# Inversion regions side by side, attention keys evacuated plainly, products spread anew, and decays in two matmuls, in a one-core hybrid encoder kernel

## The chip, the cores and the metric

The kernel runs on one core of a Trainium2 chip. The engines that matter are TensorE (PE, with its weight loads shown as PEld), VectorE (DVE), ScalarE (ACT), GpSimd (POOL) and SyncE (SP), whose queue issues nearly all DMAs. Each engine takes its instructions in order. The metric is the device time in microseconds, the median over runs.

## The reference

One encoder layer on a prompt of 1024 tokens and a sample of 256 (1280 tokens, NB = 10 blocks of 128, or 20 chunks of 64), model width 1024, float32. The normed input goes through one projection, whose columns feed three groups of heads; their gated outputs are concatenated and projected back:

```python
xn = rms_norm(h, norm_g)
proj = xn @ w_in          # a_qkv, gates, beta, alpha | b_q, b_k, b_v | c_q, c_k, c_v
qkv = silu(centred_dwconv(a_qkv, conv_w))                 # 5 taps
o_a = gated_delta_rule(...) + flip_t(gated_delta_rule(flipped ...))   # 6 heads, both directions
o_b = retention(...) + flip_t(retention(flipped ...))     # 6 heads, both directions
o_c = window_attention(q, k, v, sink)                     # 4 heads, 2 KV heads, window 128, ALiBi, sink
mix = concat([norm(o_a) * silu(gate_a), norm(o_b) * silu(gate_b), o_c * silu(gate_c)])
h = h + mix @ w_out
h = h + (p @ w_ple) * sigmoid(h @ w_pg);  y = rms_norm(h, final_g)

def gated_delta_rule(q, k, v, beta, g):                   # chunks of 64
    decay = cumsum(g)
    gamma = exp(where(incl, decay_i - decay_j, -inf))
    t_mat = where(strict, (k*beta) @ k.T * gamma, 0) + eye(64)
    u, w = triangular_solve(t_mat, [v*beta, k*beta*exp(decay)])
    # scan over chunks: state, o = step(state, u, w, q @ k.T * gamma, ...)
```

## The kernel before, in words

**Dense products.** A product takes 128 columns of `w_in` against all 1280 tokens. Activations and weights are split in a high and a low part (`xh`, `xl`, `whi`, `wlo`), and each of the 5 groups of 256 tokens takes 8 × 3 matmuls, 120 in all. There are nine for the convolution and 21 others, named in lists: `cq0 cq1 ck cv` for attention, `q k v` 0 to 2 for retention, and the numbers 0 to 7 for gate columns (`GCOL`). Each is evacuated in blocks of 512, 512 and 256 tokens. `plain` copies a block to a slot of `ot`, a tile of eight slots [128, tokens] used again and again. `evg` makes a gate: ACT copies the block to `sz` (L477), makes its sigmoid in three activations into `sg` (L99–L101), DVE multiplies them, and for gates 0 to 5 a DMA on SP stores `sg` in DRAM (`gd`). `evk` splits the keys `ck` out of PSUM into `kst`, two tiles with high and low part, six ACT copies and six DVE subtractions.

**Preparation.** `prep_stream` runs over the token blocks 9 to 0. For each it makes a Gram matrix, transposes the keys and, for each direction d, the decays: `SD[i]`, four rows of selectors, spreads the decay values in `dj` over 128 rows, and for i = 0 a further matmul with an identity (`identR`) adds the mask `MB[d]` of −1e30. Six exponentials on ACT follow (`ge`), then products on DVE and stores to DRAM (`agd`, `ad`, `l2d`).

**Inversion.** After five blocks (group g = 1, then g = 0) `invert(g)` inverts the triangles of 32 × 32 of both directions at once: it loads them from `agd` into two slots of `ot`, `IREG[d]`, runs 31 steps of DVE operations (L88, `ot<-ot` on 120 rows), ends with a memset (L426), and stores the inverses (`yd`). The access pattern of each operation spans both regions, with the stride between them.

**Joins and scan.** A join reads five chunks' inverses back (`yn`, `an`), transposes them (`xn`, L671), and completes the 64 × 64 inverses with two rounds of small matmuls (`sb<-xn,an`, then `p1s`, then `sb<-yn,p1s`). There are four for each group; its tiles have one buffer. Joins 0 to 3 belong to g = 1, joins 4 to 7 to g = 0. Then 20 scan steps for both directions (`step`, ending in `os`, L752), and norms of finished blocks.

**What sets the order.** The streams yield estimated times, and `spread` and `weave` interleave their emission: preparation and both inversions with the products in `PP`; then `PA`; then joins and scan, woven with `fill`: ten blocks of attention with `PB`, then retention (`kv(p)`, `av(p)`) with the products in `RS`. A list scheduler with a simulated timeline (`TCARGS`) makes each engine's final queue from that emission order, the dependences and the buffers. When everything is emitted up to the last scan step, the final products with `w_out`, `w_pg` and `w_ple` follow.

```python
PP = ["cq0", "cq1", 6, 7, 3, 4, 0, 5, "cv", 1, 2]
PA, PB = ["ck"], ["q0", "k0"]
RS = [["v0"], ["q1"], ["k1", "v1"], ["q2"], ["k2", "v2"], [], []]
...
for _ in spread((10 * T_PREP + 2 * 32.2, prep_stream()), length(PP)):
...
yield from spread((10 * T_AT, attn_stream()), length(PB))
```

Of the kernel before, what the change touches and what calls it, by code (L numbers as in the profile page):

```python
# [33 lines left out]
KG, MG = (), ()  # L34
AO = tuple(range(NB))
X2, SPN = 4, 0
PP = ["cq0", "cq1", 6, 7, 3, 4, 0, 5, "cv", 1, 2]
PA, PB = ["ck"], ["q0", "k0"]
RS = [["v0"], ["q1"], ["k1", "v1"], ["q2"], ["k2", "v2"], [], []]
T_PREP = 10.0  # L40
YB, VB, KB, QB = 1, 2, 1, 1
QLB = 1
SLOPE = [2.0 ** (-2 * (h + 1)) for h in range(4)]
NEG = -30000.0
XB = 6
# [7 lines left out]
def encoder_kernel(ctx: ExitStack, tc: tile.TileContext, I, O, dbg=None, upto=99):  # L53
# [27 lines left out]
    def pt_(shape, name, dt=F32):  # L81
        return pc.tile(list(shape), dt, name=name)
# [4 lines left out]
    def tt(eng, out, a, b, op):  # L87
        eng.tensor_tensor(out=out, in0=a, in1=b, op=op)  # L88
# [155 lines left out]
                        pattern=pat, channel_multiplier=cm)  # L244


    identR = pt_([128, 128], "identR", F32R)
    S.copy(identR, ident)
    MRbd, MB = [], []
    for d in range(2):  # L250
        t2 = ot[:, 7, 256 + 128 * d:384 + 128 * d]
        sel(t2, onesbd, ALU.is_ge, 0.0, 0, 2 * d - 1, [[1 - 2 * d, 128]])
        MRbd.append(t2)
        t = tmpp.tile([128, 64], F32, name=f"mbtmp{d}")
        tt(V, t, t2[:, 0:64], t2[:, 64:128], ADD)
        m = pt_([128, 64], f"mb{d}", F32R)
        V.tensor_scalar(out=m, in0=t, scalar1=-1.0, scalar2=1e30, op0=ADD, op1=MUL)
        MB.append(m)

    SD = [pt_([4, 128], f"sd{i}", F32R) for i in range(2)]  # L260
    for i in range(2):
        for l in range(2):
            for h in range(2):
                nc.gpsimd.dma_start(out=SD[i][2 * l + h:2 * l + h + 1], in_=onesbd[64 * (h ^ i):64 * (h ^ i) + 1])

# [123 lines left out]
    def plain(dst, eng=S, scale=None):  # L389
        def evac(p, t0, n):  # L390
            if scale is None:
                S.copy(dst[:, t0:t0 + n], p[:, :n])  # L392
            else:
                S.activation(out=dst[:, t0:t0 + n], in_=p[:, :n], func=AF.Copy, scale=scale)
        return evac

    IREG = (0, 3)

    def invert(g):
        for d in range(2):
# [58 lines left out]

    kreg = {}


    def evk(pp, t0, w):
        s = slice(t0, t0 + w)
        for i, (a, b) in enumerate(((T, B), (B, T))):
            S.copy(kst[i][a, s], pp[a, :w])
            tt(V, kst[i][b, s], pp[a, :w], kst[i][a, s].bitcast(F32), SUB)

    def product(n):
        if n in GCOL:
            def evg(pp, t0, w):
                o = ot[:, n, t0:t0 + w]
                sg = o if n >= 6 else gp.tile([128, 512], F32, tag="sg", name=nm("sg"))[:, :w]
                zt = gp.tile([128, 512], F32, tag="sz", name=nm("sz"))[:, :w]
                S.copy(zt, pp[:, :w])  # L477
                sigmoid(sg, zt)
                tt(V, sg, sg, zt, MUL)
                if n in GD:  # L480
                    nc.sync.dma_start(out=GD[n][:, t0:t0 + w], in_=sg)
                elif n < 3:
                    tt(V, o, o, sg, MUL)
            return [(GCOL[n], 128)], evg
        if n[0] == "c":

            return {"cq0": ([(3096, 64), (3224, 64)], plain(ot[:, 4, :], scale=cols[:, 54:55])),
                    "cq1": ([(3160, 64), (3288, 64)], plain(ot[:, 5, :], scale=cols[:, 55:56])),
                    "ck": ([(3352, 128)], evk),
                    "cv": ([(3480, 128)], plain(ot[:, 1, :]))}[n]  # L490
        p = int(n[1])
        col, dst = {"q": (1560, ot[:, 3 + p, :]), "k": (1944, kreg.get(p, ot[:, 0, :])), "v": (2328, ot[:, 1, :])}[n[0]]
        return [(col + 128 * p, 128)], plain(dst)

    PSEQ = PP + PA + PB + [n for r in RS for n in r]

    def prods(*names):
        for n in names:
# [6 lines left out]
    with tc.tile_pool(name="pa", reuse_waits="tile", bufs=2) as pa:  # L505
        kq = pa.tile([128, 3, 2, NT], F32, name="kq", bufs=1)
        SEGS = ((0, 1024, 0), (1024, 256, 1028))
        for z in range(2):
            for a0, a1 in ((0, 2), (1026, 1030), (1286, 1288)):
                G.memset(ot[:, 3 * z, a0:a1], 0.0)  # L510
# [60 lines left out]
        def prep_stream():  # L571
            for b in reversed(range(NB)):
# [16 lines left out]
                    for h, rw in ((1, T), (0, B)):  # L589
                        S.copy(kc[rw, r], kt3[64 * r:64 * r + 64, :, 64 * h:64 * h + 64])  # L590
                for d in range(2):
                    dj = pa.tile([4, 6, 64], F32R, tag="dj", name=nm("dj"))
                    for l in range(2):
                        nc.gpsimd.dma_start(out=dj[2 * l:2 * l + 2], in_=DRD[d][6 * b:6 * b + 6, l].rearrange("n (s t) -> s n t", s=2))
                    djf = dj.rearrange("r n t -> r (n t)")
                    ge = pa.tile([128, 2, 2, 3, 64], F32, tag="ge", name=nm("ge"))
                    for i in range(2):
                        pd = ps("sb")
                        mm(pd[:, 0:384], SD[i], djf, stop=bool(i))
                        if i == 0:  # L600
                            mm(pd[:, 0:384].rearrange("p (n t) -> p n t", n=6), identR, bc(MB[d].unsqueeze(1), [128, 6, 64]), start=False)
                            for n in range(6):
                                S.activation(out=ge[:, 0, n // 3, n % 3], in_=pd[:, 64 * n:64 * n + 64], func=AF.Exp,
                                             bias=negd[:, d, 2 * b + n // 3, n % 3:n % 3 + 1])
                        else:
                            S.activation(out=ge[:, 1].rearrange("p c q t -> p (c q t)"), in_=pd[:, 0:384], func=AF.Exp)
                    at = pa.tile([128, 2, 3, 2, 33], F32, tag="at", name=nm("at"), bufs=AB)
                    l2 = pa.tile([128, 2, 3, 3, 64], F32, tag="l2", name=nm("l2"))
                    last = 63 if d == 0 else 0
                    gl = ge[:, 0, :, :, last:last + 1]  # L610
                    el = ge[:, 1, :, :, last:last + 1]
                    S.copy(at[:, :, :, :, 32], bc(nbeta[:, d, 2 * b:2 * b + 2, :].unsqueeze(3), [128, 2, 3, 2]))
# [12 lines left out]
                    nc.sync.dma_start(out=ADD_[d][b // 5][2 * b % 10:2 * b % 10 + 2].rearrange("c p q w t -> p c q w t"), in_=at)
                    nc.sync.dma_start(out=L2D[d][b].rearrange("r p q a t -> p r (q a t)"),
                                      in_=l2.rearrange("p r q a t -> p r (q a t)"))
                    yield T_PREP / 2
# [10 lines left out]
        wp_cm.__exit__(None, None, None)  # L639
        return  # L640


    pc_cm.__exit__(None, None, None)
    gp_cm.__exit__(None, None, None)

    sp_cm = tc.tile_pool(name="sc", bufs=2, side="right", reuse_waits="tile")
    sp = sp_cm.__enter__()
# [135 lines left out]
    cb_cm = tc.tile_pool(name="cb", reuse_waits="tile", bufs=2)  # L783
    cb = cb_cm.__enter__()
    kst = [cb.tile([128, NT], F32R, name=f"kst{i}", bufs=1) for i in range(2)]
    bias = cb.tile([128, 384], F32, name="bias", bufs=1)
    iot = cb.tile([128, 384], mybir.dt.int32, tag="pr", name="iot", bufs=4)
    G.iota(iot, pattern=[[1, 384]], base=-128, channel_multiplier=-1)
# [12 lines left out]
            V.tensor_scalar(out=t[o, h:h + 2], in0=ident[o].unsqueeze(1).to_broadcast([64, 2, 128]), scalar1=0.0, scalar2=None, op0=MUL)  # L801

    def attn_stream():
        cvc = ot[:, 1, :]
        cvt = ot[:, 1, 0:NT].rearrange("p (b e) -> p b e", b=NB)
        for b0 in range(0, NB, 4):
            n = min(4, NB - b0)
            pt = ps("tr")
# [272 lines left out]
    def fill():  # L1081
# [15 lines left out]

        for _ in scan:
            pass
        wp_cm.__exit__(None, None, None)  # L1100
        fr = ctx.enter_context(tc.tile_pool(name="fr", bufs=1, reuse_waits="tile", side="right"))
        wraw.append(fr)
        wbuf.append(fr)
# [4 lines left out]
            cm.__exit__(None, None, None)  # L1108

    av = None  # L1110
    for _ in prods(*PA):
        pass

    scan = scan_stream()
    for _ in weave((0.0, scan), (T_LEAD, fill())):
# [103 lines left out]
```

## Time and profile before

| | |
|---|---|
| median of 3 runs | 1114.16 us (1112.15 to 1116.02) |
| the profiled execution | 1116.26 us, its span 1114.6 us |
| busy, share of the span | PE 1059.6 us (95%), DVE 638.1 (57%), ACT 522.3 (47%), POOL 268.8 (24%) |
| mean granted TensorE clock | 0.947 |
| DMA | 120.90 MB, mean 108 GB/s |
| largest PE groups | three dense forms of 1200 matmuls, 347 to 349 us each, 290 ns each |

Busy times of pipelined matmuls overlap and their ends are modelled, so a PE that is 95% busy isn't PE at its peak; the granted clock shows where it pauses. A row of the timeline gives start, duration, engine, line, operation, tiles and shape, and in brackets the idle time before it with what ended it. A row of groups has the count, the busy time, the mean in ns, and after the second bar the idle time before the group's instructions by releaser. A row of the DMA issues has count, size and the median us from issue to landing.

### The profile page before, as it was taken

The page shows a single profiled execution, that of the slowest core. Times are in us where ns is not written, and L with a number is a line of the kernel's source. Part 1 is how long each engine was busy: PE and PEld are TensorE (multiplying, and loading weights), DVE is VectorE, ACT ScalarE, POOL GpSimd, SP SyncE. Part 2 cuts the span into 40 slices and gives each one's busy share as a digit, 9 for nine tenths or more (in the row PEclk, how much of TensorE's full clock was granted, in tenths as well). Part 3 has the DMA queues.
Part 4 walks back from the last instruction along what each step waited for, and adds up shares of the span by engine and source line. Part 5 has one row for each costly group of instructions (what it writes and reads, how often), then busy time and mean ns, then how long its engine had stood idle before and what let it go on. Part 6 is the DMA issues. An engine that isn't in the chain of part 4 may idle for free.

```text
span 1114.6 us, 26117 instructions
## 1 busy us (share of the span) xinstructions
PE 1059.6 (95%) x10369; PEld 963.9 (86%) x10369; DVE 638.1 (57%) x1369; ACT 522.3 (47%) x1261; POOL 268.8 (24%) x430
## 2 busy tenths in 40 slices
PE   5999999999999888999999899999989999999996
PEld 4979999988988887888788788887769999999996
DVE  6666677574998498466644565576765123411125
ACT  7566775675665333344523522334242012455554
POOL 2011000021011121131321424457362111223421
PEclk9999999998999898899969999999559999999999
DMA  8012212467385733543543433446557232101003
GB/s 269 20 44 68 55 28 62 110 162 197 94 210 163 157 122 69 111 108 95 134 126 87 107 88 97 135 115 197 151 164 220 83 118 82 43 1 49 11 39 152
DMA packets 201429, 120.90 MB, mean 108 GB/s; under 512 B 105043, under 2 KB 186235, under 8 KB 201307
## 3 DMA queue, kind: packets, MB, share of 16 engines
q1 hardware_dynamic: 196410, 118.97, 39.0%
q8 instruction: 82, 1.34, 0.5%
q0 software_dynamic: 4896, 0.27, 0.4%
q14 instruction: 41, 0.33, 0.1%
HBM read 76.26 MB, written 42.91 MB: 107 GB/s over the span
## 4 chain that ended last, share of the span: by engine, by line
PE 51%; DVE 7%; DMA 3%; POOL 2%; issue 2%; ACT 1%; SPq 0%; POOLq 0%; DVEq 0%; ACTq 0%
PE mm L85 22%; PE sa L85 15%; PE sb L85 7%; PE tr L85 3%; DVE ot L88 2%; PE tr L849 1%; POOL oo L88 1%; PE tr L1161 1%; DMA an<-ad 1%; DVE ot L967 1%; DMA yn<-yd 1%; PE tr L948 1%; DMA vt<-vtd 1%; DMA oo<-od 1%; PE sa L1033 1%
## 5 line engine op out<-in xcount | busy, mean ns | idle before, releaser
L85 PE MATMUL mm<-xh,whi 128*128 128x256 f32 x1200 | 349.0, 291 | 9.3 <-ACT ot L392 5.6
L85 PE MATMUL mm<-xl,whi 128*128 128x256 f32 x1200 | 347.7, 290 | 0.0
L85 PE MATMUL mm<-xh,wlo 128*128 128x256 f32 x1200 | 346.5, 289 | 0.0
L85 PEld LDWEIGHTS mm<-xh,whi 128*128 128x128 f32 x1200 | 232.2, 194 | 15.4 <-ACT ot L392 5.8
L85 PEld LDWEIGHTS mm<-xl,whi 128*128 128x128 f32 x1200 | 232.2, 194 | 4.7 <-issue 2.8
L85 PEld LDWEIGHTS mm<-xh,wlo 128*128 128x128 f32 x1200 | 232.0, 193 | 3.6 <-issue 1.9
L88 DVE TENSOR_TENSOR ot<-ot 128x1284 f32<-128x1284 f32 (+16 forms) x131 | 84.3, 644 | 20.6 <-ACT ot L101 9.9
L85 PE MATMUL mm<-whi,xl 128*128 128x256 f32 x320 | 90.8, 284 | 0.0
L85 PE MATMUL mm<-whi,xh 128*128 128x256 f32 x320 | 90.8, 284 | 0.0
L85 PE MATMUL mm<-wlo,xh 128*128 128x256 f32 x320 | 90.8, 284 | 0.0
L85 PE MATMUL sa<-whi,xh 128*128 128x256 f32 x320 | 90.6, 283 | 0.0
L85 PE MATMUL sa<-whi,xl 128*128 128x256 f32 x320 | 90.2, 282 | 0.0
L85 PE MATMUL sa<-wlo,xh 128*128 128x256 f32 x320 | 90.1, 282 | 0.0
L88 DVE TENSOR_TENSOR sgm<-sb,sgm 128x256 f32<-128x256 f32 x40 | 16.9, 424 | 94.0 <-ACT sgm L101 73.8
L85 PEld LDWEIGHTS mm<-whi,xh 128*128 128x128 f32 x320 | 60.9, 191 | 0.0
L85 PEld LDWEIGHTS mm<-whi,xl 128*128 128x128 f32 x320 | 60.6, 190 | 0.0
L85 PEld LDWEIGHTS mm<-wlo,xh 128*128 128x128 f32 x320 | 60.6, 189 | 0.0
L85 PEld LDWEIGHTS sa<-whi,xh 128*128 128x128 f32 x320 | 60.3, 188 | 0.0
L85 PEld LDWEIGHTS sa<-whi,xl 128*128 128x128 f32 x320 | 60.2, 188 | 0.0
L85 PEld LDWEIGHTS sa<-wlo,xh 128*128 128x128 f32 x320 | 60.1, 188 | 0.0
L88 POOL TENSOR_TENSOR wlo<-raw,whi 128x2048 fp32r<-128x2048 f32 x7 | 33.2, 4744 | 102.2 <-ACT whi L1075 99.0
L85 PE MATMUL sa<-sv,l 128*64 128x64 f32 (+1 forms) x912 | 49.9, 242 | 7.9 <-DVE sv L88 3.5
(295 smaller groups left out, 2160.1 us busy)
## 6 DMA issues: line engine op xcount, KB each, us to landing
raw<-in_w_in SPq DMA_DIRECT2D x28, 512.0 KB, 3.8
l2d<-l SPq DMA_DIRECT2D x20, 576.0 KB, 5.0
l<-l2d SPq DMA_DIRECT2D x40, 288.0 KB, 3.1
xt<-in_x_prompt SPq DMA_DIRECT2D x8, 512.0 KB, 6.7
x<-in_x_prompt SPq DMA_DIRECT2D x32, 128.0 KB, 2.3
raw<-in_w_pg SPq DMA_DIRECT2D x4, 1024.0 KB
yp<-ot SPq DMA_DIRECT2D x8, 512.0 KB, 2.6
ad<-at SPq DMA_DIRECT2D x20, 198.0 KB, 3.1
```

The source lines that it names most:

```text
L85: nc.tensor.matmul(out, lhsT, rhs, start=start, stop=stop)
L88: eng.tensor_tensor(out=out, in0=a, in1=b, op=op)
L849: nc.tensor.transpose(pt[:, k * 128:(k + 1) * 128], pr[:, k * 128:(k + 1) * 128], ident)
L948: nc.tensor.transpose(pt[:, 0:128], bk[:, b * 128:(b + 1) * 128], ident)
L967: V.scalar_tensor_tensor(out=st[r, b2, h], in0=st[r, b, h], scalar=gs[r, 2 * p + h:2 * p + h + 1], in1=kvt[r, b, h], op0=MUL, op1=ADD)
L1033: nc.tensor.transpose(pt[:, p * 128:(p + 1) * 128], ob[:, 2 * p:2 * p + 2].rearrange("p h e -> p (h e)"), ident)
L1161: nc.tensor.transpose(pt[:, k * 128:(k + 1) * 128], hb[:, b, (n * 4 + k) * 128:(n * 4 + k + 1) * 128], ident)
```

## The change

It does five things.

1. The products are listed anew: `ck` and `cv` come into the middle of `PP`, gates 1 and 2 leave it for `PB`, `k0`, `q2` and others move within `RS`, and `PA` is gone.
2. `IREG` is (0, 1) instead of (0, 3). `cv` is evacuated to slot 2 instead of 1.
3. `ck` is evacuated plainly to slot 3; `kst` is made from there later, by the same six copies and six subtractions.
4. The decays take two matmuls. `SD` has 128 rows (the selectors in rows 0 to 3, in `SD[0]` the identity twice in rows 64 to 127), and `DJ[d]`, one persistent tile for each direction, has the mask in rows 64 to 127.
5. `sg` and `sz` have one buffer each (`SGB = 1`) instead of two, and their pool stays open until the scan's end.

```diff
-PP = ["cq0", "cq1", 6, 7, 3, 4, 0, 5, "cv", 1, 2]
-PA, PB = ["ck"], ["q0", "k0"]
-RS = [["v0"], ["q1"], ["k1", "v1"], ["q2"], ["k2", "v2"], [], []]
+PP = ["cq0", "cq1", 6, 7, 3, "ck", "cv", 4, 0, 5]
+PB = [1, 2, "q0"]
+RS = [["k0", "v0"], ["q1"], ["k1", "v1"], ["k2"], ["v2"], ["q2"], []]
...
+SGB = 1
...
-    SD = [pt_([4, 128], f"sd{i}", F32R) for i in range(2)]
+    SD = [pt_([128, 128], f"sd{i}", F32R) for i in range(2)]
     for i in range(2):
+        V.tensor_scalar(out=SD[i], in0=ident, scalar1=0.0, scalar2=None, op0=MUL)
+        if i == 0:
+            for h in range(2):
+                S.copy(SD[i][64:128, 64 * h:64 * h + 64], ident[64:128, 64:128])
...
-    IREG = (0, 3)
+    IREG = (0, 1)
...
-                sg = o if n >= 6 else gp.tile([128, 512], F32, tag="sg", name=nm("sg"))[:, :w]
-                zt = gp.tile([128, 512], F32, tag="sz", name=nm("sz"))[:, :w]
+                sg = o if n >= 6 else gp.tile([128, 512], F32, tag="sg", name=nm("sg"), bufs=SGB)[:, :w]
+                zt = gp.tile([128, 512], F32, tag="sz", name=nm("sz"), bufs=SGB)[:, :w]
...
-                    "ck": ([(3352, 128)], evk),
-                    "cv": ([(3480, 128)], plain(ot[:, 1, :]))}[n]
+                    "ck": ([(3352, 128)], plain(ot[:, 3, :])),
+                    "cv": ([(3480, 128)], plain(ot[:, 2, :]))}[n]
...
+        DJ = [pa.tile([128, 6, 64], F32R, name=f"dj{d}", bufs=1) for d in range(2)]
+        for d in range(2):
+            V.tensor_scalar(out=DJ[d][0:64], in0=..., scalar1=0.0, scalar2=None, op0=MUL)
+            V.tensor_scalar(out=DJ[d][64:128], in0=bc(MRbd[d][64:128, 64:128].unsqueeze(1), [64, 6, 64]),
+                            scalar1=-1.0, scalar2=1e30, op0=ADD, op1=MUL)
...
-                    dj = pa.tile([4, 6, 64], F32R, tag="dj", name=nm("dj"))
...
-                        mm(pd[:, 0:384], SD[i], djf, stop=bool(i))
+                        mm(pd[:, 0:384], SD[i], DJ[d].rearrange("r n t -> r (n t)"))
                         if i == 0:
-                            mm(pd[:, 0:384].rearrange("p (n t) -> p n t", n=6), identR, bc(MB[d].unsqueeze(1), [128, 6, 64]), start=False)
...
+    for t0, w in NBLK:
+        s = slice(t0, t0 + w)
+        for i, (a, b) in enumerate(((T, B), (B, T))):
+            S.copy(kst[i][a, s], ot[a, 3, s])
+            tt(V, kst[i][b, s], ot[a, 3, s], kst[i][a, s].bitcast(F32), SUB)
```

The order moves on all engines. First PE's queue at the decays of one block in the second half of the preparation, before (numbers behind the tiles' names count their instances):

```order
L586 MATMUL tr_315_3538<-ident_74,kq_460 128x128 x3
L85 MATMUL sb_319_3551<-dj_317_3547,sd0_336 128x384
L85 MATMUL sb_319_3551<-mb0_329,identR_324 128x384
L85 MATMUL sb_320_3560<-dj_317_3547,sd1_337 128x384
L85 MATMUL mm_323_3582<-xh_88,whi_293_3202 128x256
```

and after:

```order
L584 MATMUL tr_296_3398<-ident_74,kq_454 128x128 x3
L86 MATMUL sb_299_3410<-dj0_455,sd0_326 128x384
L86 MATMUL sb_300_3418<-dj0_455,sd1_327 128x384
L86 MATMUL mm_306_3446<-xh_88,whi_283_3200 128x256
L86 MATMUL mm_306_3446<-xl_89,whi_283_3200 128x256
```

The matmul of the mask is gone, and both others have 128 rows.

Next PE's queue at the first join, before. `mm_484` and `mm_521` belong to the product `q0`, and 21.4 products stand ahead of the join:

```order
L85 MATMUL mm_484_5112<-xl_89,whi_451_4873 128x256
L85 MATMUL mm_484_5112<-xh_88,wlo_452_4874 128x256
L85 MATMUL sb_488_5176<-xn2_487_5174,an_485_5162 32x32 x30
L85 MATMUL mm_521_5416<-xh_88,whi_451_4873 128x256
L85 MATMUL mm_521_5416<-xl_89,whi_451_4873 128x256
```

and after, where `mm_409` is the last of product 5, the 19th, `mm_440` the first of product 1, and `pts` and `pr` belong to the first attention block:

```order
L86 MATMUL mm_409_4576<-xh_88,wlo_390_4249 128x256
L86 MATMUL tr_431_4738<-pts_428_4730,ot_90 64x128
L86 MATMUL tr_431_4738<-pts_430_4736,ot_90 64x128
L86 MATMUL tr_431_4738<-pts_428_4730,ot_90 64x128
L86 MATMUL tr_431_4738<-pts_430_4736,ot_90 64x128
L848 MATMUL tr_432_4745<-ident_74,pr_424_4711 128x128 x2
L86 MATMUL sb_446_4839<-xn2_445_4837,an_443_4825 32x32 x22
...
L86 MATMUL sb_448_4873<-yn_444_4832,p1s_447_4840 32x32
L86 MATMUL mm_440_4768<-xh_88,whi_401_4434 128x256
```

The first join has moved ahead of products 1, 2 and q0, with the first attention block ahead of it. At the first join of g = 0 the count of products ahead went from 23.66 to 22.02, at the last one from 24.0 to 23.31.

Last, DVE's queue in the second inversion (`ot<-ot 120x...` are its steps), before:

```order
L88 TENSOR_TENSOR ot<-ot 120x2x84
L88 TENSOR_TENSOR ot<-ot 120x2x3x28
L88 TENSOR_TENSOR ot<-ot 120x2x108
L88 TENSOR_TENSOR ot<-ot 120x2x4x27
L88 TENSOR_TENSOR ot<-ot 120x2x130
```

and after:

```order
L89 TENSOR_TENSOR ot<-ot 120x2x84
L89 TENSOR_TENSOR wlo_4765<-raw_4762,whi_4764 128x1024
L89 TENSOR_TENSOR ot<-ot 120x2x3x28
L89 TENSOR_TENSOR sg_4487<-sg_4487,sz_4488 128x512
L89 TENSOR_TENSOR p1s_4840<-sb_4839,nbeta 32x480 x2
L89 TENSOR_TENSOR ot<-ot 120x2x108
L89 TENSOR_TENSOR ot<-tr_4756,ot 128x128
L89 TENSOR_TENSOR ot<-ot 120x2x4x27
```

Operations of joins 0 to 3, attention blocks, gates and the first two scan steps now stand between the steps of the second inversion, where nearly only its own stood.

More of the change, by code (lines that the diff above doesn't have):

```diff
@@ L244, in sel @@
                         pattern=pat, channel_multiplier=cm)
-    identR = pt_([128, 128], "identR", F32R)
-    S.copy(identR, ident)
-    MRbd, MB = [], []
+    MRbd = []
     for d in range(2):
@@ L253, in encoder_kernel @@
         MRbd.append(t2)
[L254 to L258, printed above, removed]
-    SD = [pt_([4, 128], f"sd{i}", F32R) for i in range(2)]
+    SD = [pt_([128, 128], f"sd{i}", F32R) for i in range(2)]
     for i in range(2):
+        V.tensor_scalar(out=SD[i], in0=ident, scalar1=0.0, scalar2=None, op0=MUL)
+        if i == 0:
+            for h in range(2):
+                S.copy(SD[i][64:128, 64 * h:64 * h + 64], ident[64:128, 64:128])
         for l in range(2):
@@ L462, in encoder_kernel @@
     kreg = {}
[L465 to L469, printed above, removed]
     def product(n):
@@ L493, in product @@
         return [(col + 128 * p, 128)], plain(dst)
-    PSEQ = PP + PA + PB + [n for r in RS for n in r]
+    PSEQ = PP + PB + [n for r in RS for n in r]
     def prods(*names):
@@ L507, in encoder_kernel @@
         SEGS = ((0, 1024, 0), (1024, 256, 1028))
+        DJ = [pa.tile([128, 6, 64], F32R, name=f"dj{d}", bufs=1) for d in range(2)]
+        for d in range(2):
+            V.tensor_scalar(out=DJ[d][0:64], in0=bc(ident[0:64, 0:64].unsqueeze(1), [64, 6, 64]), scalar1=0.0, scalar2=None, op0=MUL)
+            V.tensor_scalar(out=DJ[d][64:128], in0=bc(MRbd[d][64:128, 64:128].unsqueeze(1), [64, 6, 64]),
+                            scalar1=-1.0, scalar2=1e30, op0=ADD, op1=MUL)
         for z in range(2):
@@ L591, in prep_stream @@
                 for d in range(2):
-                    dj = pa.tile([4, 6, 64], F32R, tag="dj", name=nm("dj"))
                     for l in range(2):
-                        nc.gpsimd.dma_start(out=dj[2 * l:2 * l + 2], in_=DRD[d][6 * b:6 * b + 6, l].rearrange("n (s t) -> s n t", s=2))
-                    djf = dj.rearrange("r n t -> r (n t)")
+                        nc.gpsimd.dma_start(out=DJ[d][2 * l:2 * l + 2], in_=DRD[d][6 * b:6 * b + 6, l].rearrange("n (s t) -> s n t", s=2))
                     ge = pa.tile([128, 2, 2, 3, 64], F32, tag="ge", name=nm("ge"))
@@ L803, in attn_stream @@
     def attn_stream():
-        cvc = ot[:, 1, :]
-        cvt = ot[:, 1, 0:NT].rearrange("p (b e) -> p b e", b=NB)
+        cvc = ot[:, 2, :]
+        cvt = ot[:, 2, 0:NT].rearrange("p (b e) -> p b e", b=NB)
         for b0 in range(0, NB, 4):
@@ L1099, in fill @@
             pass
-        wp_cm.__exit__(None, None, None)
+        for cm in (gp_cm, wp_cm):
+            cm.__exit__(None, None, None)
         fr = ctx.enter_context(tc.tile_pool(name="fr", bufs=1, reuse_waits="tile", side="right"))
@@ L1110, in encoder_kernel @@
     av = None
-    for _ in prods(*PA):
-        pass
     scan = scan_stream()
```

1 line of the change is left out of this document (removed).

## The prediction

> **What bounds the kernel now.** I read first the page's busy shares (PE 95%, DVE 57%, ACT 47% of a span of 1114.6 us), which name TensorE, and then the busy time by stretches, which shows whether a busy PE is at its peak.
>
> ```profile
> core 0: us, PE busy (x) PEld busy (x) DVE busy (x) ACT busy (x) POOL busy (x), PEclk, DMA share, GB/s
> 214.00:269.00 55.00, 52.13 (x375) 43.93 (x374) 36.97 (x89) 34.28 (x111) 11.11 (x26) 0.91 0.66 172
> 269.00:366.00 97.00, 92.13 (x746) 82.80 (x744) 85.50 (x180) 58.13 (x162) 12.88 (x30) 1.00 0.59 159
> 366.00:430.00 64.00, 58.63 (x505) 57.93 (x506) 48.41 (x93) 25.74 (x50) 10.39 (x20) 0.92 0.49 122
> 430.00:525.00 95.00, 91.51 (x1243) 77.27 (x1243) 58.95 (x170) 40.36 (x104) 20.64 (x36) 0.93 0.46 104
> 525.00:575.00 50.00, 46.72 (x768) 37.29 (x769) 30.96 (x93) 21.23 (x57) 14.66 (x23) 0.82 0.57 137
> 575.00:763.00 188.00, 184.32 (x2215) 159.88 (x2216) 107.29 (x308) 64.04 (x180) 70.46 (x127) 0.99 0.39 105
> 763.00:829.00 66.00, 57.69 (x598) 43.34 (x596) 46.84 (x115) 22.73 (x64) 39.44 (x52) 0.64 0.55 158
> 829.00:1115.00 286.00, 276.35 (x2311) 274.41 (x2311) 84.91 (x155) 111.29 (x278) 73.82 (x55) 0.98 0.26 85
> ```
>
> The granted clock (the column after POOL) separates them. In 575–763 and from 829 on it is 0.98–0.99: dense matmuls follow one another, and only fewer matmuls help. In 525–575 (joins 5 to 7 of the second group, no dense product left beside them) it is 0.82 and in the tail 763–829 it is 0.64: PE does short matmuls and waits for other engines. In 269–366 DVE too is nearly full, 85.5 of 97 us: decays, and the first inversion with 10 products.
>
> The timeline shows how the stretches hang together. First the end of the first inversion (the memset L426):
>
> ```profile
> 365.93 0.11 DVE L426 MEMSET ot<- 120x64 f32 x1
> 366.08 1.07 ACT L392 COPY ot<-mm 128x512 f32<-128x512 f32 x2 [3.51 <-DVE ot L426]
> 366.72 0.58 PE L85 MATMUL mm<-xh,whi 128*128 128x256 f32 x1 [5.59 <-ACT ot L392]
> 367.09 0.41 PE L85 MATMUL mm<-xl,whi 128*128 128x256 f32 x1
> 367.31 0.41 PE L85 MATMUL mm<-xh,wlo 128*128 128x256 f32 x1
> 372.49 0.28 PE L85 MATMUL mm<-xh,whi 128*128 128x256 f32 x1
> 372.61 0.28 PE L85 MATMUL mm<-xl,whi 128*128 128x256 f32 x1
> ```
>
> The product cv is evacuated into ot[:,1], which lies between the inversion's regions 0 and 3, so ACT holds it until the inversion ends; PE stands 5.59 us. Afterwards its matmuls come 0.22 us apart instead of 0.12. A product is 120 matmuls, so 120 × 0.12 = 14.4 us at full pace.
>
> Then the path to the joins (`xn,an` is a join's first product; `p1s` its next step):
>
> ```profile
> 366.07 5.19 SPq L428 DMA_DIRECT2D yd<-ot  x2
> 383.78 4.37 DVE L88 TENSOR_TENSOR ot<-ot 120x2048 f32<-120x2048 f32 x2 [6.83 <-DMA ot<-agd]
> 389.14 0.68 DVE L671 STREAM_TRANSPOSE xn<-yn 128x480 f32<-128x480 f32 x1
> 428.32 1.14 PE L85 MATMUL sb<-xn,an 32*32 32x32 f32 x60
> 440.08 0.11 DVE L426 MEMSET ot<- 120x64 f32 x1
> 523.84 1.14 PE L85 MATMUL sb<-xn,an 32*32 32x32 f32 x60
> 576.15 1.32 DVE L88 TENSOR_TENSOR p1s<-sb,nbeta 32x480 f32<-32x480 f32 x2
> ```
>
> The first join's operand xn is ready at 389.8, but its matmuls run at 428.3, since 1, 2, ck and a part of q0 stand ahead of them on PE's in-order queue. The second inversion is over at 440, its first join (join 4) comes at 523.8, and join 7 at 576.2. It is this order, and not data, that sends the last joins late and leaves the scan's end uncovered in the tail.
>
> **The decays.** Ten blocks × two directions, each now with three matmuls:
>
> ```profile
> 330.41 0.28 PE L85 MATMUL mm<-xh,wlo 128*128 128x256 f32 x1
> 330.62 0.44 PE L85 MATMUL sb<-dj,sd 4*128 4x384 f32 x1
> 330.99 0.44 PE L85 MATMUL sb<-mb,identR 128*128 128x384 f32 x1
> 331.36 0.43 PE L85 MATMUL sb<-dj,sd 4*128 4x384 f32 x1
> 331.73 0.39 PE L85 MATMUL mm<-xh,whi 128*128 128x256 f32 x1
> ```
>
> From 330.41 to 331.73 is 1.32 us, less the dense matmul's own 0.12: 1.20 us. Two of the same pace would cost 0.80 (saving 0.40 a direction, 8 us in 20); two at the pace of neighbours, 0.12 us per 256 columns, cost 2 × 0.18 = 0.36 (saving 0.84, 17 us). All steps here are slow that lead into, out of or between shapes, and the change leaves no 4-row shape; I take 0.65, so 13 us of PE queue. The Trainium skill, "TensorEngine Tiling (Array Packing)", Key Properties, says that changing the tiling mode drains TensorE; by it the saving would be the 17, and the 0.37 us steps between 4-row and 128-row matmuls agree with it. Five of the ten blocks lie in 269–366, where DVE's 85.5 us stay; there the PE gain only pays for other PE work. The other five are worth up to 6 us in 214–269, which also waits for stores (DMA share 0.66): I take 4. The selectors' fills (six short DVE fills for five operations) lie at the start, where PE computes convolutions; nothing. The 40 small loads into DJ keep their number on POOL's queue, and one buffer for each direction is as deep as two buffers that the directions took in turn: nothing.
>
> **Keys and region.** Six ACT copies and six DVE subtractions for kst move from the queue after the first inversion to inside it, with the first attention block and cv's transposes. On DVE that is 6 × 0.4–0.7 = 3.6 us for kst and about 6 us for the block, 9–10 against DVE's idle 11.5 us in 269–366; part fits, and I let the inversion's end slip by 4. With the 4 gained before, it stays at 366. PE: by 372.2 it had 18 products done; it needs 19 and one attention block before the first join: 372.2 + 14.4 + 5 − 13 − 5.6 (the gap removed) = 373. (The 5 is an estimate: 8 score matmuls at 0.18 and 36 short ones at about 0.1 us.) It then waits for xn: 366 + 23 (as now) = 389. So about 16 us of idleness take the place of the 5.6, because product 1 stands behind the first join. The Trainium skill, "TensorE: Matmul & The Clock Gate", Why this matters, warns against PE pauses over about 3 us, after which the clock halves. The 0.22 us steps after 5.59 us agree; by rule and rows alike the first 5 us after this wait run at half pace, 2–3 us, which I count in the next term.
>
> **The second inversion and the joins.** It starts as now at 384 and now shares DVE with four joins, two scan steps and more attention blocks.
>
> ```profile
> 383.70:440.30 56.60, 49.86 (x495) 48.24 (x494) 54.20 (x103) 21.17 (x42) 8.55 (x16) 0.97 0.35 93
> L835 DVE CUSTOM_DVE_ANT_0 pr<-sb,bias,snk 128x384 f32<-128x384 f32 x24 | 14.5, 616 | 13.5 <-PE sb L85 11.0 <-PE tr L849 2.3
> L88 DVE TENSOR_TENSOR p1s<-sb,nbeta 32x480 f32<-32x480 f32 x16 | 10.4, 653 | 2.5 <-PE sb L85 2.1
> ```
>
> DVE is busy 54.2 of the 56.6 us (third pair of columns). By the new order it gets six more p1s (3.9), eight score maxima of 384 columns for four of 256 (+3), their scalings (+2.4), three transposes (2), scan operations (4.4), two more gates and more gate columns (2.2), v adds and the rest (3), and sheds kst (−3.6): 54.2 + 17 to 21 = 71–75, with waits some 82. So it ends at 466 and join 4 could follow at 480. PE from 389: before, 5.86 products (84 us; counted in the order, as all such fractions) lay between 366 and join 4, of 150 us of busy time (58.6 + 91.5); the other 66 stay less one block (5), and the products are 3.02: 43.5 + 61 = 104.5 us, done at about 489 with part of the clock pause in it (the busy 66 includes latency that dense work now covers). PE is the later of the two. Joins 4 to 7 took 52 us, for want of buffers rather than of PE: join 7 at 489 − 3 + 52 = 538, **38 us earlier than 576**.
>
> Against this more stands behind join 7: 6.69 products instead of 6.0 (+10) and an attention block more (+5). Net −23 for the middle.
>
> **The tail.**
>
> ```profile
> 767.75 0.30 ACT L752 COPY os<-sa 128x192 f32<-128x192 f32 x1
> ...
> 803.08 0.32 ACT L752 COPY os<-sa 128x192 f32<-128x192 f32 x1 [1.34 <-PE sa L85]
> 826.77 0.90 PE L1033 MATMUL sa<-ident,oo 128*128 128x128 f32 x3 [1.02 <-DMA oo<-ond]
> 827.33 0.78 PE L85 MATMUL mm<-whi,xh 128*128 128x256 f32 x2
> ```
>
> Now 3.5 scan steps follow the last product (it ends at 763; the two rows are the first and last of eight `os` copies, one for each step and direction, so 35.3 us for 3.5 steps, 10 a step), and the norms' round trip lasts until 826. After the change two steps follow; 1.5 steps fewer would be −15, but kv(2) moves wholly behind the scan and costs some of it: −10. One more av(2) block is left for the final product: +4. Net −6. The 286 us of the final products stay.
>
> **One gate buffer.**
>
> ```profile
> L477 ACT COPY sz<-mm 128x512 f32<-128x512 f32 x16 | 9.4, 589 | 28.3 <-PE mm L85 25.1 <-DVE sg L88 3.2
> L99 ACT ACTIVATE sg<-sz 128x512 f32<-128x512 f32 x12 | 7.6, 635 | 5.5 <-DMA gd<-sg 5.3
> L100 ACT ACTIVATE sg<-sg,cols 128x512 f32<-128x512 f32 x12 | 8.8, 730 | 0.3
> L101 ACT ACTIVATE sg<-sg 128x512 f32<-128x512 f32 x12 | 7.6, 632 | 0.3
> gd<-sg SPq DMA_DIRECT2D x12, 256.0 KB, 7.8
> ```
>
> With one sg, a block's sigmoid waits until the block before has landed: 0.64 + 0.73 + 0.63 + about 0.7 (the product with sz) + 7.8 = 10.5 us a wide block. A product in 269–366 takes about 20 us, of which a wide block is 0.4, or 8 us. ACT then stands about 2.5 us a wide block, and everything behind it (the decays' exponentials, exps of the scores) too. ACT has 39 us idle of these 97. The bounds are nothing (if it all falls into that idle time) and 8 × 2.5 = 20 us for the eight wide blocks there; with two buffers ACT already loses 5.3 us. I take **+5**. On SP's queue the six stores of gates 1 and 2 now stand among the joins' yn and l2d loads; a store that waits for its product on DVE holds these back, 0 to 6 × 0.7 us, inside the joins' 52 us.
>
> **Sum** against the profiled execution's 1116.3: −23 − 6 + 5 = −24, so 1092; the median of the three runs (1114.2) lies 2 lower, so **1090 us**. As a cross-check by counts: 13 us of decays less, and 11 from stretches where the granted clock is 0.64–0.82.
>
> **Rivals.**
> *Only the work counts* (17 in 100). Joins and scan fill the time that the products leave and hardly overlap; then PE's shorter queue (8 to 17 us) is all, less 3 for the new pause: about 1104. For it: 93–98% busy from 430 to 763. Against it: the clock of 0.82 and 0.64.
> *The gate buffer decides* (13 in 100; the other side). Where ge's exponentials stand behind the held sigmoid, the DVE work of a block starts late, so the whole preparation lengthens. At the dense pace a wide block comes every 5.8 us; 12 wide blocks × (10.5 − 5.8) = 56 us at most; with 45 of it on the path the time is 1090 − 5 + 45 = 1130. It decides once over some 29 us of waits reach the path, that is 2.4 us a wide block. The Trainium skill, "Trainium Kernel Development and Optimization", Best Practices, asks for double buffers to overlap DMA with compute, which speaks for this rival; the trace shows only the 5.3 us with two.
> *The gain is eaten by DVE* (8 in 100). If inversion 1 slips by the whole 10 and inversion 2 takes 105 us rather than 82 because its chain waits in order for scores and joins, join 4 comes at 513, and the 15 us of work moved behind it leave 1114: no change.
>
> **How the numbers follow.** The forecast has 58 in 100, with 1066 to 1111 as its own range: below, DVE's and PE's ends meet at 475, the tail gives 16 and the buffer nothing; above, 20 for the buffer. 4 remain for a better end than that. 0.3%, or 3.3 us, is about what can be told from no change. Faster: 58 + 17 + 4 = 79; same 8; slower 13. The range 1066 to 1118 leaves out the 4 and the 13.
>
> **What would show it.** In the profile after: no `mb,identR` rows and steps of about 0.2–0.25 us around `dj,sd`; the 5.59 us row gone and a PE wait of some 16 us for xn; the second inversion's memset at about 466 instead of 440; join 7's p1s near 538; 6.7 products behind it; a tail at under 60 us. A larger ACT wait for `gd<-sg` than 30 us with prep's end past 375 would show the gate rival; a second inversion beyond 490, the DVE one.

## The result, and the profile after

The changed kernel takes 1100.49 us (median of 4 runs, 1097.21 to 1103.77), the kernel before in the same comparison 1114.02. The ratio is 0.9892, 95% interval [0.9864, 0.9920]: 12 us faster by the ratio (9 to 15 by its interval), where 24 were forecast: inside the range, at half the size. The profiled execution is the fastest of the four (1097.21 us, span 1095.5); its trace is 19 us shorter than that of before.

The busy time by stretches, with columns as before:

```profile
core 0: us, PE busy (x) PEld busy (x) DVE busy (x) ACT busy (x) POOL busy (x), PEclk, DMA share, GB/s
258.00:370.00 112.00, 93.53 (x777) 89.34 (x776) 95.53 (x203) 60.70 (x174) 25.32 (x47) 0.94 0.60 161
370.00:397.00 27.00, 20.69 (x201) 18.99 (x199) 13.36 (x28) 10.26 (x24) 5.60 (x3) 0.82 0.52 99
397.00:490.00 93.00, 87.78 (x1213) 78.05 (x1213) 77.47 (x186) 47.68 (x110) 19.88 (x27) 0.96 0.51 124
490.00:544.00 54.00, 54.00 (x874) 46.23 (x870) 31.05 (x90) 22.08 (x58) 13.87 (x21) 1.00 0.54 130
544.00:760.00 216.00, 213.11 (x2588) 183.99 (x2588) 125.74 (x363) 74.84 (x212) 87.86 (x156) 0.98 0.44 118
760.00:800.00 40.00, 31.15 (x358) 22.81 (x356) 30.93 (x77) 16.04 (x44) 20.63 (x26) 0.83 0.53 157
```

Joins 5 to 7 (490–544) run under dense products: PE busy throughout at a granted clock of 1.00, where it was 0.82. But PE is idle 18.5 us in 258–370; before had 8.5 from 213 to the first xn. Over the whole span PE stands 69.3 us without a matmul, 54.9 before: the gain is not less idle time. PE's busy time is 33 us shorter (1026.2 us for 1059.6); the two-matmul decays account for about 17 of it, and the rest goes with a higher granted clock (0.970 for 0.947), which is not separated further. The path to the joins, in the timeline:

```profile
370.23 0.11 DVE L424 MEMSET ot<- 120x64 f32 x1
391.62 0.68 DVE L664 STREAM_TRANSPOSE xn<-yn 128x480 f32<-128x480 f32 x1
464.76 0.11 DVE L424 MEMSET ot<- 120x64 f32 x1
489.81 1.35 DVE L89 TENSOR_TENSOR p1s<-sb,nbeta 32x480 f32<-32x480 f32 x2
542.90 1.33 DVE L89 TENSOR_TENSOR p1s<-sb,nbeta 32x480 f32<-32x480 f32 x2 [2.05 <-PE sb L86]
```

The rows are the first inversion's end, the first join's xn, the second inversion's end, and p1s of joins 4 and 7. Join 7 comes 33 us earlier; the span shrinks by 19. The table sets the stations side by side, from the traces (times in us; the third column is the run e11 below). "Idle" is time without any matmul on PE.

| | before | after | e11 |
|---|---|---|---|
| PE idle from 213 to the first xn | 8.5 | 26.8 | 14.7 |
| first xn | 389.1 | 391.6 | 384.2 |
| join 7's p1s; products ahead of it | 576.2; 24.05 | 542.9; 23.31 | 530.7; 23.94 |
| last product (30th) ends | 763.4 | 760.3 | 757.0 |
| scan steps after it | 4.0 | 2.0 | 1.0 |
| last `os` | 803.1 | 774.6 | 762.9 |
| span | 1114.6 | 1095.5 | 1082.3 |

Most of what PE loses in the preparation is in these rows, two totals of PE's waits first (us, times, longest):

```profile
PE sb L86 <- ACT ge L598: 10.3, 7, 3.5
PE sb L86 <- DVE xn L664: 4.0, 1, 4.0
284.90 1.07 PE L86 MATMUL sb<-dj,sd 128*128 128x384 f32 x2 [3.47 <-ACT ge L598]
363.48 0.79 PE L86 MATMUL sb<-kst,qlz 128*128 128x256 f32 x2 [4.34 <-DVE qlz L89]
367.32 0.59 ACT L468 COPY sz<-mm 128x512 f32<-128x512 f32 x1 [6.07 <-DVE sg L89]
366.61 0.68 DVE L89 TENSOR_TENSOR sg<-sg,sz 128x512 f32<-128x512 f32 x1
367.96 0.55 PE L86 MATMUL sb<-kst,qh 128*128 128x256 f32 x1 [3.69 <-ACT sz L468]
ACT sg L100 <- DMA gd<-sg: 20.2, 10, 4.2
ACT sz L468 <- DVE sg L89: 16.4, 10, 6.1
```

The largest share, 10.3 us (0.4 before), is the decays' matmuls waiting for the exponentials `ge` on ACT, whose queue holds the gates' sigmoids too; the longest such wait is the third row. The first attention block stands on PE's queue and waits 4.34 us for its operand, which DVE makes behind kst and the inversion's last steps. The gate's product (366.61) stands further back on DVE; until it is done the single sz is taken, ACT's copy waits 6.07 us, and PE 3.69. The last two rows are totals of the waits: 20.2 us for gate stores (it was 6.9 in the trace of before) and 16.4 for the gate's product. Such totals don't price the buffer: in e10, with two buffers, ACT waits 18.5 us for the stores.

The first xn stands on DVE's queue behind this row:

```profile
387.84 3.87 DVE L89 TENSOR_TENSOR ot<-ot 120x2048 f32<-120x2048 f32 x1 [4.27 <-DMA ot<-agd]
```

It is the second inversion's first multiply, which waits for its triangles to be loaded; xn (391.62) follows it without a pause.

### The profile page after: what moved, and what is told of

Same layout as the page of the kernel before. It is cut to its first block, busy times and chain, and to the rows that moved or that the text cites. A ratio compares the mean times of both kernels' runs of the same rounds, so it can differ in the third digit from the quotient of the medians.

```text
span 1095.5 us, 26088 instructions
## 1 busy us (share of the span) xinstructions
PE 1026.2 (94%) x10349; PEld 945.3 (86%) x10349; DVE 639.4 (58%) x1371; ACT 523.4 (48%) x1265; POOL 278.3 (25%) x430
## 4 chain that ended last, share of the span: by engine, by line
PE 52%; DVE 9%; DMA 6%; issue 2%; SPq 2%; ACT 1%; POOL 0%; DVEq 0%; ACTq 0%; POOLq 0%
PE mm L86 23%; PE sa L86 16%; PE sb L86 7%; PE tr L86 3%; DVE ot L89 2%; DMA yd<-ot 1%; DVE ot L966 1%; PE tr L848 1%; DMA yn<-yd 1%; DVE l L89 1%; PE tr L1159 1%; DMA ad<-at 1%; DMA ot<-agd 1%; DVE sg L89 1%; SPq L618 1%
## 5 line engine op out<-in xcount | busy, mean ns | idle before, releaser
L86 PEld LDWEIGHTS mm<-xh,whi 128*128 128x128 f32 x1200 | 231.2, 193 | 10.3 <-ACT sz L468 3.7
L89 DVE TENSOR_TENSOR ot<-ot 128x1284 f32<-128x1284 f32 (+16 forms) x131 | 86.7, 661 | 19.2 <-ACT ot L102 9.9
L525 DVE SCALAR_TENSOR_TENSOR ot<-ot,cols 128x1284 f32<-128x1284 f32 x36 | 55.9, 1552 | 0.5
```

The lines of the kernel that those rows point to most:

```text
L86: nc.tensor.matmul(out, lhsT, rhs, start=start, stop=stop)
L525: V.scalar_tensor_tensor(out=Y[:, 0:1284], in0=R[:, j:j + 1284], scalar=cw(ti, j), in1=Y[:, 0:1284], op0=MUL, op1=ADD)
```

## The experiments

Theory A was that the order carries the gain and the crowding at the first inversion's end gives some back; theory B that only PE's shorter queue counts. Every edit lets the scheduler draw all queues anew, so each run changes its part and, a little, everything else. Runs were compared in several groups, in which the kernel before took 1110 to 1115 us, so ratios to it are compared; 0.001 is 1.1 us.

| run | ratio to before | 95% interval |
|---|---|---|
| the change | 0.9892 | 0.9864 to 0.9920 |
| e1 change, two gate buffers | 0.9812 | 0.9781 to 0.9843 |
| e2 change, products spread as before | 0.9997 | 0.9974 to 1.0020 |
| e3 change, old decays | 0.9979 | 0.9956 to 1.0001 |
| e4 change, regions 0 and 3 | 1.0156 | 1.0123 to 1.0188 |
| e5 before, new decays | 1.0023 | 1.0001 to 1.0045 |
| e6 before, one gate buffer | 1.0127 | 1.0092 to 1.0162 |
| e7 e1, kst on GpSimd | 0.9908 | 0.9876 to 0.9941 |
| e8 e1, gate product on GpSimd | 0.9883 | 0.9841 to 0.9925 |
| e9 before, regions side by side | 1.0032 | 1.0009 to 1.0055 |
| e10 before, regions and decays | 0.9894 | 0.9867 to 0.9920 |
| e11 e1, inverses stored whole | 0.9761 | 0.9735 to 0.9788 |
| e12 e11, direction 1 first | 0.9759 | 0.9730 to 0.9789 |

**The gate buffer: e1 and e6.** In e1 the gates of the preparation have two buffers again, in a pool that is replaced by a small one ahead of the joins.

```diff
+    gbuf = [2]
...
-                sg = o if n >= 6 else gp.tile([128, 512], F32, tag="sg", name=nm("sg"), bufs=SGB)[:, :w]
+                sg = o if n >= 6 else gp.tile([128, 512], F32, tag="sg", name=nm("sg"), bufs=gbuf[0])[:, :w]
...
+    gp_cm.__exit__(None, None, None)
+    gp_cm = tc.tile_pool(name="gp2", bufs=1, side="right", reuse_waits="tile")
+    gp = gp_cm.__enter__()
+    gbuf[0] = 1
```

> The changed kernel with two buffers of sg and sz during the preparation (one from the first join on, since two don't fit there). Theory A (the order carries the gain; the single buffer and DVE's crowded queue at the end of the first inversion give some of it back): ACT's waits for the gate stores fall from 20.2 us to under 10, product 5 ends some 5 us earlier than 387, and the time falls by 4 to 8 us from 1100. Theory B (only the number of matmuls on PE counts): PE's queue holds the same work, so 1100, no change.

In e6 the kernel before gets `bufs=1` for sg and sz.

> The kernel before with one buffer of sg and sz instead of two. Two buffers in the changed kernel gained 8.9 us. Theory A: the six gates' wide blocks cost 1 to 2 us each wherever DVE and ACT are crowded, and before has four gates there and two behind the inversion: slower by 4 to 10 us. Rival: the cost arises only where kst and the first attention block crowd DVE in the first inversion, which before doesn't have: within 3 us of before.

e1 is faster than the change by 0.0080 (8.9 us, with an error of some 4.6), e6 slower than before by 0.0127 (14 us), more than the 4 to 8 and 4 to 10 expected: the single buffer costs in both kernels, so the rival, which tied it to the new crowd on DVE, falls, and B with it. In e1 product 5 ends at 370 instead of 387, and PE's idle time in 258–370 falls from 18.5 to 7.2 us; its waits for `ge` fall from 10.3 to 5.3. The first join comes no earlier for it (p1s at 396.5, 396.7 in the change), as PE then waits 7.3 us for xn; instead 19.8 products are done ahead of the join, for 19.0. ACT's waits for the stores, in e1 (under 10 expected) and in e6:

```profile
ACT sg L100 <- DMA gd<-sg: 11.7, 6, 3.7
```

```profile
ACT sg L99 <- DMA gd<-sg: 26.5, 13, 9.3
```

**The spread: e2.** `PP`, `PB` and `RS` as before, with ck at the end of `PP`.

> The changed kernel with the products spread as before (gates 1 and 2 in the preparation, ck at its end, then q0 k0 and so on). Theory A: the first join again stands behind 21 to 22 products, the last join's p1s goes back from 543 to 560-575, and the time is 1106 to 1112. Theory B: the same matmuls, so 1100.

All of the gain is gone (0.9997), and B falls again, since the matmuls are the same. The first join's p1s is back at 426, though its xn is ready at 388.9, and join 7's at 577:

```profile
426.21 1.33 DVE L89 TENSOR_TENSOR p1s<-sb,nbeta 32x480 f32<-32x480 f32 x2
...
576.95 1.33 DVE L89 TENSOR_TENSOR p1s<-sb,nbeta 32x480 f32<-32x480 f32 x2 [1.45 <-PE sb L86]
```

With e10 (below: old spread, two buffers) the runs make a table of two by two, all with the new regions and decays: old spread 0.9894 with two gate buffers and 0.9997 with one, new spread 0.9812 and 0.9892. The new spread gains 0.0082 or 0.0105, the single buffer costs 0.0103 or 0.0080. The old spread with two buffers also splits `ck` straight out of PSUM; the plain evacuation was not run alone, and the table leaves little for it.

**The decays: e3 and e5.** e3 puts the three matmuls back into the change, e5 puts the two into the kernel before.

```diff
...
-                        mm(pd[:, 0:384], SD[i], DJ[d].rearrange("r n t -> r (n t)"))
+                        mm(pd[:, 0:384], SD[i], djf, stop=bool(i))
                         if i == 0:
+                            mm(pd[:, 0:384].rearrange("p (n t) -> p n t", n=6), identR, bc(MB[d].unsqueeze(1), [128, 6, 64]), start=False)
```

> The changed kernel with the three matmuls of the decays (four-row selectors, identity times mask) put back. Theory A: of the 13 us of PE time by my sum some 4 to 8 reach the end, since DVE is nearly full in the second half of the preparation: 1104 to 1108. Theory B: all 13 come back, 1113, which would be the whole gain.

> The kernel before with the decays alone changed to two matmuls of 128 rows. Putting the old decays back into the changed kernel cost 9.7 us. If the decays are worth the same by themselves (fewer matmuls on PE), the time falls by 8 to 12 us from before. If their worth depends on the new order (PE ahead of DVE in the second half of the preparation), it falls by 2 to 5, as before's cv stands waiting for the inversion there anyway.

e3 loses 0.0087 (9.7 us), between its two theories; e5 gains nothing, outside both of its own. The matmuls themselves are shorter everywhere. PE in the changed kernel:

```profile
318.22 0.28 PE L86 MATMUL mm<-xh,whi 128*128 128x256 f32 x1
318.34 0.34 PE L86 MATMUL sb<-dj,sd 128*128 128x384 f32 x1
318.51 0.28 PE L86 MATMUL mm<-xl,whi 128*128 128x256 f32 x1
```

The step in takes 0.12 us and the step out 0.17 for 384 columns, the pace of dense matmuls (0.12 for 256): two cost 0.35 us for 1.20, so 0.85 a direction and 17 us in 20. That the 4-row shape itself is slow, and not only the mask's matmul, is shown where one such matmul stands alone between dense ones in the trace of before:

```profile
217.18 0.28 PE L85 MATMUL mm<-xh,whi 128*128 128x256 f32 x1
217.39 0.44 PE L85 MATMUL sb<-dj,sd 4*128 4x384 f32 x1
217.75 0.38 PE L85 MATMUL mm<-xl,whi 128*128 128x256 f32 x1
```

From 217.18 to 217.75 it is 0.57 us, less 0.12 for the dense one: 0.45, where the 128-row matmul takes 0.17. In e5 the row of cv's wait, 5.59 us before, shows where it went:

```profile
362.47 0.58 PE L85 MATMUL mm<-xh,whi 128*128 128x256 f32 x1 [11.59 <-ACT ot L389]
```

PE reaches cv some 10 us sooner, the inversion, which DVE sets, ends only 4 us sooner (361.7), and the wait is 6 us longer. The rest of the saving is lost in other waits: up to the first xn PE is idle 22.0 us for 8.5, some 5 of it on `ge`.

**The regions: e4, e9 and e10.** e4 sets `IREG = (0, 3)` in the change, with ck in slot 1.

> The changed kernel with the inversion's regions in slots 0 and 3 again, ck then in slot 1 and cv in slot 2, both between the regions. Theory A: what lies between the regions is held until the inversion ends at 366-370, so ck and cv are evacuated only then, PE stands for 10 to 30 us, the first attention block moves behind it, and the time is 1110 to 1125. If neighbouring regions matter for nothing: 1100.

1.0156, slower than before and somewhat more than expected: without this part the change loses. ck and cv now lie between the regions, ACT's copy is held until the inversion ends (355), and PE stands 27.8 us:

```profile
355.05 1.07 ACT L390 COPY ot<-mm 128x512 f32<-128x512 f32 x2 [17.90 <-DVE ot L424]
355.69 0.58 PE L86 MATMUL mm<-xh,whi 128*128 128x256 f32 x1 [27.82 <-ACT ot L390]
```

e9 gives the kernel before the neighbouring regions alone, e10 these and the decays.

```diff
-    IREG = (0, 3)
+    IREG = (0, 1)
-                    "cv": ([(3480, 128)], plain(ot[:, 1, :]))}[n]
+                    "cv": ([(3480, 128)], plain(ot[:, 2, :]))}[n]
...
```

> The kernel before with the regions side by side (slots 0 and 1) and cv in slot 2, nothing else changed. Theory A: cv's wait of 5.6 us and the half clock behind it (about 2.5 us) go, and since PE's queue of products is what the first join then waits for, the time falls by 5 to 8 us from before (ratio 0.993 to 0.995). Rival (the wait was cover for other work that is late anyway): within 2 us.

> The kernel before with regions side by side, cv in slot 2, and the decays in two matmuls. The decays alone gave nothing, and there cv waited 11.6 us for the inversion instead of 5.6. Theory A: the decays' PE time was only turned into a longer wait for the regions, so both together give more than the sum of each: 12 to 18 us less than before (ratio 0.984 to 0.989). Rival (the parts add): the regions' 5 to 8 us alone, ratio 0.993 to 0.995.

e10 comes out in theory A's direction, just short of its 0.984 to 0.989: each part alone gains nothing (1.0023 and 1.0032), both together 0.0106, as much as the whole change. e9 is a miss. cv's wait is gone there (PE idle 1.1 us from 213 to the first xn), and the first join comes 12 us earlier; but this lead is lost by join 4. Its p1s of joins 0 and 4:

```profile
420.21 1.33 DVE L88 TENSOR_TENSOR p1s<-sb,nbeta 32x480 f32<-32x480 f32 x2
...
525.54 0.65 DVE L88 TENSOR_TENSOR p1s<-sb,nbeta 32x480 f32<-32x480 f32 x1 [0.36 <-PE sb L85]
```

Join 4 was at 525.0 before. The new queue puts 25.40 products ahead of join 7 instead of 24.05, so the time went into products that were not yet urgent. After join 7 fewer remain beside the scan: PE is idle 12.1 us until the last product (3.7 before), and that product ends at 763.7 as before. In e10, with 25.38 ahead, join 7 comes at 564.9 and the last product ends at 757.2. Why the scheduler drew e9 so and not otherwise wasn't tried.

**Relieving DVE: e7 and e8**, on top of e1. In e7 the six subtractions of kst go to GpSimd, in e8 the gates' product.

```diff
-            tt(V, kst[i][b, s], ot[a, 3, s], kst[i][a, s].bitcast(F32), SUB)
+            tt(G, kst[i][b, s], ot[a, 3, s], kst[i][a, s].bitcast(F32), SUB)
```

```diff
-                tt(V, sg, sg, zt, MUL)
+                tt(G if n in GD else V, sg, sg, zt, MUL)
```

> The changed kernel with two gate buffers in the preparation, and the six subtractions of kst on GpSimd instead of VectorE. If DVE's crowded queue sets the end of the first inversion (367 in the run with two buffers), it comes 3 to 4 us earlier and the time falls by 2 to 4 us from 1091. If GpSimd's slower subtraction (about 1.3 us for 512 columns by the nearest row, for 0.69) delays the first attention block instead, 1091 to 1094.

> The changed kernel with two gate buffers in the preparation, and the product sg times sz of the stored gates on GpSimd. It takes 12 x 0.68 + 6 x 0.42 = 10.7 us off DVE, so if DVE sets the preparation the time falls by 4 to 8 us from 1091. If GpSimd's queue holds the product behind elc and the joins' products, which wait for other engines, the sz buffers are held longer: 1091 to 1097.

Both are slower than e1, by 0.0096 and 0.0071, more than either side expected. The inversion doesn't end earlier (369.5 and 370.0; 366.9 in e1), though DVE has less to do, and the first xn comes at 396.0 and 395.5 instead of 389.9; in e7 join 7 then lies 9 us later (554.0 for 545.3), in e8 it lies at 543.1 with 0.6 products fewer ahead of it. Why the inversion ends 3 us later stays open. The rest of xn's delay stands in the redrawn queues. SP in e7:

```profile
369.96 1.03 SPq L426 DMA_DIRECT2D yd<-ot  x1
371.09 4.88 SPq L473 DMA_DIRECT2D gd<-sg  x1
376.03 0.92 SPq L426 DMA_DIRECT2D yd<-ot  x1
```

A gate's store now stands between the two stores of inverses (in e8 two, 5.03 us), and the triangles' load, on which DVE's next multiply waits, comes later: 19.7 and 18.7 us from the inversion's end to that multiply, 17.5 in e1. This also bounds what a single run shows: redrawn queues may move a time by several us, so the 9 us of e1 and of e3 rest on their pairs too (e6 for the buffer; for the decays e10 against e9, which lacks only them: 0.0138).

**The way from the inversion to the joins: e11 and e12**, on top of e1. Behind the inversion's end the triangles' load stands on SP behind the two stores, and xn on DVE behind that load. SP's queue in e1 behind 366.9 (start, duration of the issue):

```profile
367.08 5.46 SPq L426 DMA_DIRECT2D yd<-ot  x2
372.64 4.19 SPq L473 DMA_DIRECT2D gd<-sg  x1
376.93 0.38 SPq L402 DMA_DIRECT2D ot<-agd  x1
```

A store of inverses skips each row's padding column, so it writes 3840 pieces of 128 B. e11 stores the 33 columns:

```diff
-    YDD = [[tc.dram_tile([120, 32, 32], F32, name=f"yd{d}_{g}") ...
+    YDD = [[tc.dram_tile([120, 32, 33], F32, name=f"yd{d}_{g}") ...
-            nc.sync.dma_start(out=YDD[d][g], in_=ot[0:120, IREG[d], 0:1056].rearrange("p (a b) -> p a b", a=32)[:, :, 0:32])
+            nc.sync.dma_start(out=YDD[d][g], in_=ot[0:120, IREG[d], 0:1056].rearrange("p (a b) -> p a b", a=32))
...
```

> The changed kernel with two gate buffers in the preparation, and the inverses stored with their padding column, so that a store writes 120 pieces of 4.2 KB instead of 3840 of 128 B. Theory A: from the first inversion's end (366.9) to the first join's xn (389.9) the 23 us are DMA, 5.5 of it SP's issue of the two stores; with few pieces xn comes at 380 to 384, and since the joins follow each other from there, the time falls by 4 to 8 us from the run with two buffers (ratio to before 0.974 to 0.978). Rival: other transfers fill the DMA engines there, or PE's queue sets the later joins: within 2 us, ratio 0.979 to 0.983.

> As the one with whole stores of the inverses, and direction 1 stored before direction 0, since the first join reads direction 1. Theory A: xn of the first join comes 1 to 3 us earlier again; time 0 to 3 us less than that run. Rival: no difference, as the second store is short by then.

SP's queue and the first xn in e11:

```profile
367.56 0.81 SPq L426 DMA_DIRECT2D yd<-ot  x2
372.31 0.32 SPq L402 DMA_DIRECT2D ot<-agd  x1
```

```profile
384.19 0.67 DVE L669 STREAM_TRANSPOSE xn<-yn 128x480 f32<-128x480 f32 x1
...
530.65 1.33 DVE L89 TENSOR_TENSOR p1s<-sb,nbeta 32x480 f32<-32x480 f32 x2 [1.80 <-PE sb L86]
```

The issue falls from 5.46 to 0.81 us, the gate's store behind it from 4.19 to 0.35, the way from the inversion's end to xn from 23.0 to 16.8, and the ratio is 0.9761: 0.0051 (5.7 us) better than e1, just clear of an error of 0.0041, and 0.0131 better than the change. Join 7 comes 14.7 us earlier, of which under half reaches the end. e12 has xn at 382.8, but only because its first inversion ends earlier (365.1): from there it is 17.7 us, so the swap didn't shorten the way. As a second drawing of the queues with whole stores it agrees with e11's time. e11 beats both kernels: 1084.06 us for 1110.18 of before in its group.

## Why the prediction was right, and where its sizes were off

**In sum.** The direction, the path and the stations to join 7 were right; the gain was half of the forecast. By the traces, join 7 came 33.3 us earlier, as forecast (38, less 5 for the buffer), and behind it 14.2 us were lost instead of 9: 19 us less, where the sum had 24. The other 7 us lie between these two traces and the medians: the trace of after is of the fastest of its four runs (3.3 us under their median), that of before of a run 2 us above its own; the medians differ by 13.5, and the ratio gives 12.

**The path to the joins held.** Forecast and measured: first xn 389 and 391.6; the second inversion's end 466 and 464.8; join 4 489 and 489.8; join 7 538 and 542.9; the 6.69 products behind it were counted in the order, so they are no forecast. The 489 stands 4.5 us below its own sum (389 + 104.5), for latency that dense work would cover, without a row for it. That the order is what moves join 7 is shown by e2, where the old spread brings it back to 577 and the time to that of before.

**Step "decays", mis-sized.** Two matmuls were priced between the pace of neighbours (17 us saved) and that of the old steps (8), and 13 was taken; 17 was measured. A lone 4-row matmul took 0.45 us where a 128-row one takes 0.17. The rule of the Trainium skill (TensorEngine Tiling (Array Packing), Key Properties) that a change of tiling mode drains TensorE agrees with this; no row names the mode. With no 4-row shape left, the 0.37 us steps are gone. That this time is worth something only if nothing holds PE afterwards was said for DVE's half of the preparation; e5 and e10 show that cv's wait, too, swallowed a part.

**Step "keys and region", wrong in PE's part.** The first inversion was let slip by 4 and made up by 4; it ended 4.3 later. The 4 made up is borne out by e5 (361.7 for 365.9), so by these the slip was 8.5; e1, at 366.9, puts 3.3 of it on the gate buffer. Product 5 was forecast to end at 373 and ended at 387. The sum had PE's work there and no new waits for ACT and DVE: the decays for `ge` (11.5 with both of its lines), sz (6.9) and the attention block (4.3). PE's idle time in 213–391.6 is 26.8 us, where the sum had 16. This cost the first join almost nothing, by slack and not by foresight: PE was to wait 16 us for xn, and still waited 4. In e1, with the gate mended, product 5 ends at 370.

**Step "one gate buffer", mis-sized.** +5 was taken from ACT's waits for the stores; 8.9 was measured (e1's error of 4.6 just reaches 5; e6's 14 does not). The price lacked the second wait: sz is held until DVE, in order and crowded, comes to the product (16.4 us of ACT's waits). The chain of a block was counted by durations, 0.7 us for the product, not by its place on DVE's queue. The rival's mechanism, exponentials held behind the gate, did appear (PE's waits for `ge`, 10.3 us for 5.3 with two buffers), but even e6's 14 us are short of the 29 at which it would have decided. The bound of 20 held both.

**Behind join 7.** From join 7 to the span's end it took 538.4 us before and 552.6 after: +14 where the sum had +15 − 6 = +9. From join 7 to the last product's end it is +30 instead of +15, and from there to the end −16 instead of −6: −26 up to the first matmul of the final products, and +10 behind it, where the forecast had 286 us stay and +4. The likely cause, which no run separates, is that the scan steps that no longer follow the last product stand among the products and cost PE time there. Before, eight `os` copies follow the last product, which is 4 steps and not 3.5, and after it 2.

**The rival "only the work counts"** gave 1104, nearer than 1090 to the 1100.5 measured, but not by its mechanism: by it e1, e2 and e4 would have been 1100. Two large effects, about 12 us for the spread and 9 against it for the buffer, nearly cancel. e10 reaches the same time with neither.

**The rival "DVE eats the gain"** didn't come about: the second inversion ran from 387.8 to 464.8, 77 us where 82 were forecast and 105 needed.

**Two slips in the working.** The upper end of its own range, 1111, doesn't follow from its terms: with 20 instead of 5 for the buffer 1090 becomes 1105. And in 269–366 PE made 4.8 products, not 10; the sum used 20 us a product there, which agrees with 4.8.

## What to carry to other kernels

Time saved ahead of a wait lengthens the wait; look for what ends last behind the saving (here a dependence that existed only because two regions spanned an unrelated slot) and remove both, or neither pays. A buffer given up is priced also by the place of its last reader on that engine's queue, not by the reader's duration alone, and by what stands behind the held engine. And where a path runs through DRAM, count the pieces of each transfer: here writing a padding column along was worth about half as much as the change.

## What the runs showed of the hardware

A store of 3840 pieces of 128 B takes 1.0 us to issue (1.03 in e7), and the DMA behind it on SP's queue took 3 to 5 us here: the second such store (two together 5.46 us in e1), and behind it a gate's store (4.19 in e1, 4.17 in the change, 0.35 in e11). With 120 pieces of 4.2 KB each, at 3% more bytes, the two stores took 0.81 us. In the prediction the 23 us between inversion and join stood as given. A 128-row matmul of 384 columns between dense ones has steps of 0.12 and 0.17 us; those with 4 rows had 0.21 to 0.37.
